# Second layer's attention: projection pieces moved to the odd steps and tied behind the scores

## The chip, the cores and the metric

The kernel runs on one core of one Trainium2 chip. The metric is device time in microseconds (us) of one execution. Engines are named as in the profile: PE (matrix multiply, PEld its weight loads), DVE (vector), ACT (scalar activation), POOL (the third elementwise engine), SP (its queue issues most DMAs).

## The reference, cut to what matters

A two-layer trunk over 512 latent tokens and 256 context tokens, width 1024. The second layer's mixer is windowed grouped-query attention with sinks: 16 query heads in 4 groups share 4 key/value heads of 64.

```python
def gqa_sink_attend(q, k, v, mask, sinks):
    ...
    s = jnp.einsum('bqkgd,bnkd->bkgqn', qg, k).astype(jnp.float32) * (HEAD_DIM ** -0.5)
    if mask is not None:
        s = jnp.where(mask, s, NEG_INF)
    ...
    p = jax.nn.softmax(jnp.concatenate([s, sink], axis=-1), axis=-1)[..., :-1]
    o = jnp.einsum('bkgqn,bnkd->bqkgd', p.astype(v.dtype), v)
    return o.reshape(B, Q, GQA_HEADS, HEAD_DIM)

def mixer_c(h_x, h_c, w_in, w_out, sinks, cos, sin, with_ctx_out):
    q_x, k_x, v_x = jnp.split(h_x @ w_in, [C_Q_COLS, C_Q_COLS + C_KV_COLS], axis=-1)
    q_x = apply_rope(heads(q_x, GQA_HEADS), cos, sin)
    ...
    out_x = block_sweep(blk, q_x).reshape(B, S, C_Q_COLS) @ w_out
```

Each block of 128 queries sees all 256 context keys and the latent keys of its own and the neighbouring blocks (256 or 384 keys).

## The kernel before, in words

Everything is kept with features on the partitions. An fp32 operand is split into a high and a low part, and a projection is three products per 128 features (`mm3`, line 205): high x high, high x low, low x high. A q projection for one pair of heads has 8 k-slices, so 24 matmuls on 512 columns; an output-projection piece over the first half of the features has 4 k-slices, so 12.

**Attention in steps.** Head pair `m` (0 to 7) and query block `i` (0 to 3) make 32 steps, `n = 4 m + i` (`gqa_step`, line 1525). A step has two parts. Part `a`, for both heads of the pair: scores on PE into a PSUM tile `s` (two buffers, one used per head; L1540 for context keys, L1542 for latent keys), mask and negated maximum on DVE (L1544), exponential with its sum on ACT (L1549), the sink's exponential (L1551), sum and reciprocal on DVE (L1553, L1554), normalising on POOL (L1557). Part `b`: transposes of the probabilities on PE into tiles `t` (L1569; a fifth block on L1581 in the middle query blocks), copies to SBUF by ACT (L1577, L1582) and DVE (L1575), and in every second step the value product for two query blocks together (`values`, L411), whose result is split into `att(m)` (L196 on ACT, L197 on DVE).

**Order.** `run_steps` (line 439) writes, for step `n`: part `a` of step `n`, part `b` of step `n - 1`, then the fillers of step `n`. So at even `n` the part `b` carries a value product, at odd `n` only transposes. The program builder decides each engine's issue order ahead of time: it plays the program through, and where an engine would be free it takes the earliest instruction of the source that is ready there. On the chip each engine then runs its list in order. `tc.issue_after(x)` makes the builder put what is written under it, on the engine of `x`, behind `x`; it sets an order and adds no wait for `x` to finish.

**Fillers.** `q_piece(m)` (line 1508) projects the queries of head pair `m`: weights from the stream `S`, `mm3` into the single PSUM tile `lin`, then rope (`rope_of`: DVE L386 and L387, POOL L388 and L389) and the split into `qs[m]` (ACT L369, DVE L372; four buffers). `first_part(t)` makes two output-projection pieces (`wo1`, L1618 adds them to the residual) over the features of head pairs 0 to 3, which are ready after step 15. Head pairs 4 to 7 write their results over `hx`, the input of the q pieces, so all q pieces come before these. Each `S.next()` loads weights (512 KB by SP), and prepares tiles up to two ahead: a cast on ACT (L158) and a subtraction on DVE (L159), into three buffers each.

The plan before spreads, per head pair, its pieces over the pair's four steps: q1 and q2 at steps 0 and 2, q3 and q4 at 4 and 6, q5 at 8, q6 at 12, q7 at 16, and the output pieces at 20, 22, 24 to 28 and 30. q0 comes before the steps. After the steps the second half of the output projection follows (four more weight tiles), then the norm and the FFN.

Of the kernel before, what the change touches and what calls it, by code (L numbers as in the profile page):

```python
# [15 lines left out]
P = 128  # L16
D = 1024
KT = D // P
NX = 512
NC = 256  # L20
# [17 lines left out]
def tile_trunk(  # L38
# [27 lines left out]
    nc = tc.nc  # L66
# [126 lines left out]
    S = Stream()  # L193

    def split(hi, lo, src, scale=1.0):
        nc.scalar.activation(hi, src, AF.Copy, scale=scale)  # L196
        return nc.vector.tensor_sub(lo, src, f32(hi))  # L197
# [4 lines left out]
        nc.gpsimd.dma_start(f32(lo), src, accum_op=ALU.add)  # L202
        nc.scalar.copy(hi, src)

    def mm3(ps, wh, wl, xh, xl, n=KT):
        for k in range(n):
            nc.tensor.matmul(ps, wh(k), xh(k), start=k == 0, stop=False)  # L207
            nc.tensor.matmul(ps, wh(k), xl(k), start=False, stop=False)  # L208
            end = nc.tensor.matmul(ps, wl(k), xh(k), start=False, stop=k == n - 1)  # L209
        return end  # L210
# [17 lines left out]
    def wslice(t, m=P):  # L228
        v = t.rearrange("p (k m) -> p k m", m=m)
        return lambda k: v[:, k, :]  # L230
# [127 lines left out]
    xh = lambda k: hx[k][:, 0, :]  # L358
    xl = lambda k: hx[k][:, 1, :]
# [76 lines left out]
    def vload():  # L436
        return [tuple(wslice(t, 256) for t in S.next()) for _ in range(2)]

    def run_steps(steps, fillers):

        prev = None
        for n, (a, b) in enumerate(steps):
            a()
            if prev:
                prev()
            prev = b
            for f in fillers[n] if n < len(fillers) else []:
                f()
        prev()

    def spread(items, n):
        out_ = [[] for _ in range(n)]
        for i, f in enumerate(items):
            out_[i * n // len(items)].append(f)
        return out_
# [172 lines left out]
    with ExitStack() as st:  # L628
# [3 lines left out]
        linp = lambda: lin.tile([P, NX], F32, tag="lin", name="lin")  # L632
# [32 lines left out]
        with ExitStack() as s0:  # L665
# [7 lines left out]
            def ada0_mm(b):  # L673
                ps = tp()
                for k in range(KT):
                    ada_mm(ps, S.next(0), k, k == 0, k == KT - 1)
                    S.request(min(S.at + 8, 2 * KT + 3))
                return ps
# [8 lines left out]
            ps = ada0_mm(0)  # L687
# [393 lines left out]
        ps = linp().rearrange("p (t c) -> p t c", t=2)  # L1081
# [47 lines left out]
        def first_part(t):  # L1129
            def f():  # L1130
                w = S.next()
                for m in (2 * t, 2 * t + 1):
                    wo_chunk(m, w, "x", 0)
                    wo_chunk(m, w, "c", 0)
            return f

        steps, fillers = [], []
# [31 lines left out]
        for t in range(4):  # L1169
            w = S.next(3)  # L1170
# [29 lines left out]
    with ExitStack() as st:  # L1200
# [17 lines left out]
        q_tile = lambda: fp.tile([P, 4 * H], F32, tag="q", name="q")  # L1218
# [198 lines left out]
        for n, sg in enumerate(supers0):  # L1417
            for p in sg:
# [9 lines left out]
                else:  # L1428
# [9 lines left out]
                    z, u = z_tile(), s_tile()  # L1438
# [14 lines left out]
    with ExitStack() as st:  # L1453
# [6 lines left out]
        linp = lambda: lin.tile([P, NX], F32, tag="lin", name="lin")  # L1460
# [11 lines left out]
        def q_tile(m, ps):  # L1472
            qs[m] = gp.tile([P, 2, NX], F32R, tag="gq", name="gq", bufs=4)
            evac_pair(qs[m], 0, NX, rope_of(ps, gp), -0.125)
# [33 lines left out]
        def q_piece(m):  # L1508
            def f():
                wh, wl = (wslice(t) for t in S.next())  # L1510
                ps = linp() if m else tp()
                mm3(ps, wh, wl, xh, xl)
                q_tile(m, ps)
            return f

        def att(m):

            if m < 4:
                return hc[2 * m], hc[2 * m + 1]
            return [hx[m][:, i, :].rearrange("p (a n) -> p a n", a=2) for i in range(2)]  # L1520
# [4 lines left out]
        def gqa_step(m, i):  # L1525
            kv = m // 2
            lo, hi = max(i - 1, 0), min(i + 1, 3)
            nk = (hi - lo + 1) * P
            d = {}

            def a():
                q = qs[m]
                small = lambda name: gp.tile([P, 2], F32, tag=name, name=name, bufs=4)
                mx, rs, es = small("mx"), small("rs"), small("es")
                pp = []
                for c in range(2):
                    ql = q[:, c, i * P : (i + 1) * P]
                    s = sps.tile([P, 1024], F32, tag="s", name="s")
                    for n, k in ((0, k1), (1, k2)):
                        nc.tensor.matmul(s[:, 256:512], ql, k[:, kv, 0:NC], start=(n == 0), stop=(n == 1))  # L1540
                    for n, k in ((0, k1), (1, k2)):
                        nc.tensor.matmul(s[:, 512 : 512 + nk], ql, k[:, kv, NC + lo * P : NC + lo * P + nk], start=(n == 0), stop=(n == 1))  # L1542
                    sv = s[:, 256 : 512 + nk]
                    nc.vector.tensor_tensor_reduce(  # L1544
                        out=sv, in0=sv, in1=gm0 if i == 0 else gm[:, 0 : 256 + nk], op0=ALU.add, op1=ALU.min,
                        scale=1.0, scalar=snk[:, 2 * m + c : 2 * m + c + 1], accum_out=mx[:, c : c + 1],
                    )
                    p = gp.tile([P, 640], F32, tag="p", name="p", bufs=5)
                    nc.scalar.activation(p[:, 0 : 256 + nk], sv, AF.Exp, bias=mx[:, c : c + 1], scale=-1.0, accum_out=rs[:, c : c + 1])  # L1549
                    sk = 2 * m + c  # L1550
                    nc.scalar.activation(es[:, c : c + 1], snk[:, sk : sk + 1], AF.Exp, bias=mx[:, c : c + 1], scale=-1.0)  # L1551
                    pp.append(p)
                nc.vector.tensor_add(rs, rs, es)  # L1553
                nc.vector.reciprocal(rs, rs)  # L1554
                for c in range(2):
                    z = pp[c][:, 0 : 256 + nk]
                    nc.gpsimd.tensor_scalar(z, z, rs[:, c : c + 1], 1.0, op0=ALU.mult, op1=ALU.mult)  # L1557
                d["p"] = pp

            def b():  # L1560
                nb = 2 + hi - lo + 1
                h = i % 2
                if h == 0:
                    turned[0] = gp.tile([P, 2, 10, P], F32, tag="pt", name="pt", bufs=1)
                pt = turned[0]
                for c in range(2):
                    t = tp((P, 4, P))
                    for k in range(4):
                        nc.tensor.transpose(t[:, k, :], d["p"][c][:, k * P : (k + 1) * P], ident)  # L1569
                    if i == 0:  # L1570
                        z, t = pt[:, c, 0:6, :].rearrange("p (a b) n -> p a b n", b=3)[:, :, 0:2, :], t.rearrange("p (a b) n -> p a b n", b=2)
                    else:
                        z = pt[:, c, 5 * h : 5 * h + 4, :]
                    if c:
                        nc.vector.tensor_copy(z, t)  # L1575
                    else:
                        nc.scalar.copy(z, t)  # L1577
                if nb == 5:
                    t = tp((P, 4, P))
                    for c in range(2):  # L1580
                        nc.tensor.transpose(t[:, c, :], d["p"][c][:, 4 * P : 5 * P], ident)  # L1581
                    nc.scalar.copy(pt[:, :, 5 * h + 4, :], t[:, 0:2, :])  # L1582
                if h == 0:
                    return
                o = tp()
                both = slice(0, 2 * P)

                def term(k, n, cols):
                    return (lambda c: v[:, k, 64 * kv : 64 * kv + 64], lambda c: pt[:, c, n, :], cols)


                values(o, [
                    term(0, slice(0, 6, 5), both),
                    *([term(i, 2, slice(0, P))] if i > 1 else []),
                    term(1 + i, slice(3, 8, 4), both),
                    term(2 + i, slice(4, 9, 4), both),
                    *([term(3 + i, 9, slice(P, 2 * P))] if i < 3 else []),
                    term(1, slice(1, 7, 5), both),
                ])
                split(*(z[:, i // 2, :] for z in att(m)), o[:, both])  # L1600

            return a, b


# [25 lines left out]
        for m in range(KT):  # L1630
# [2 lines left out]
        super_weights(1, type("", (), {"tile": lambda self, *a, **k: spool[0].tile(*a, **k)})())  # L1633
        q_piece(0)()
        steps, fillers = [], []
        plan = {
            0: [q_piece(1), q_piece(2)], 1: [q_piece(3), q_piece(4)], 2: [q_piece(5)], 3: [q_piece(6)], 4: [q_piece(7)],
            5: first_part(0), 6: first_part(1) + first_part(2), 7: first_part(3),
        }
        for m in range(8):  # L1640
            steps += [gqa_step(m, i) for i in range(4)]
            fillers += spread(plan[m], 4)
        run_steps(steps, fillers)
        held = []
        for t in range(4):
            w = S.next(0 if t >= 2 else 2)
# [336 lines left out]
```

## Time and profile before

| what | us |
|---|---|
| median of 3 runs | 1601.86 |
| lowest, highest | 1600.62, 1605.14 |
| the profiled execution | 1608.56 |
| its span | 1606.8 |
| mean granted PE clock in it | 0.991 |
| first scores to end of the last value product, in it | 1039.4 to 1216.6 |

The profiled execution is a run of its own, and its time stands beside the median of others. In the table by windows each row gives a stretch, then for each engine the busy time and the number of instructions, then the granted PE clock (1.00 is full), the DMA share and GB/s. A timeline row gives start, duration, engine, line, operation, tiles (out<-in), count, and in brackets the idle time before it with what ended it. A waits row says who waited on which line for whom: total us, times, longest. A groups row gives line, engine, tiles, shapes, count, then busy us and mean ns of one, then idle time before.

### The profile page before, as it was taken

To read this page: it belongs to the slowest core of one execution; us is meant where nothing else is said; L and a number is where in the kernel's file an instruction comes from. 1 tells how busy PE (TensorE), PEld (TensorE's weight loads), DVE (VectorE), ACT (ScalarE), POOL (GpSimd) and SP (SyncE) were. 2 spreads that over 40 slices of the span, in tenths; PEclk is the share of its full clock that TensorE was granted. 3 is DMA by queue.
4 is the path that set the end of the run, shared out by engine and by line. 5 is a ranking of instruction groups with operands and counts; after the bars stand their busy time and mean duration, and the time that the engine had idled before them with its cause. 6 is when DMAs were issued, how large, how long until landed. Compare 5 with 4: busy or idle time off the path is not lost.

```text
span 1606.8 us, 25479 instructions
## 1 busy us (share of the span) xinstructions
PE 1541.8 (96%) x9854; PEld 1377.4 (86%) x9854; DVE 1242.9 (77%) x2125; ACT 734.1 (46%) x1276; POOL 275.9 (17%) x311
## 2 busy tenths in 40 slices
PE   5899999999999999999999999999998999999997
PEld 3798888877878998999999998886777899989897
DVE  4667798966698789879798867677766987869686
ACT  4346545445344413434424254466664543525354
POOL 2222223463010000010100001354331000000001
PEclk9999999999999999999999999999999999999999
DMA  9312354543145465485866652320011442423321
GB/s 348 100 53 70 99 157 136 182 128 101 63 132 158 118 173 155 133 221 154 213 183 162 201 146 71 106 66 27 15 40 54 131 144 68 131 72 100 118 80 53
DMA packets 68577, 195.28 MB, mean 122 GB/s; under 512 B 6772, under 2 KB 19220, under 8 KB 68456
## 3 DMA queue, kind: packets, MB, share of 16 engines
q1 hardware_dynamic: 58824, 161.26, 31.5%
q0 software_dynamic: 9056, 31.87, 9.4%
q8 instruction: 78, 1.28, 0.3%
q10 hardware_dynamic: 576, 0.52, 0.1%
q14 instruction: 43, 0.35, 0.1%
HBM read 160.45 MB, written 4.86 MB: 103 GB/s over the span
## 4 chain that ended last, share of the span: by engine, by line
PE 52%; DVE 5%; DMA 4%; issue 4%; ACT 1%; POOL 0%; DVEq 0%; POOLq 0%; ACTq 0%; SPq 0%
PE f L1764 4%; PE f L1763 4%; PE f L1762 4%; PE f L1334 4%; PE f L1333 4%; PE f L1332 4%; PE f L1374 3%; PE f L1375 3%; PE f L1373 3%; PE t L411 2%; PE f L1815 2%; PE f L1817 2%; PE f L1816 2%; DMA wl<-raw 2%; PE t L1569 2%
## 5 line engine op out<-in xcount | busy, mean ns | idle before, releaser
L196 ACT ACTIVATE wh<-raw 128x1024 fp32r<-128x1024 f32 (+1 forms) x96 | 92.3, 978 | 232.4 <-DVE raw L540 106.6
L207 PE MATMUL lin<-hb,wh 128*128 128x512 f32 (+1 forms) x456 | 162.1, 356 | 8.3 <-DVE rbuf L387 2.1
L208 PE MATMUL lin<-hb,wh 128*128 128x512 f32 (+1 forms) x456 | 160.3, 351 | 1.0 <-DVE hb L1106 0.7
L209 PE MATMUL lin<-hb,wl 128*128 128x512 f32 (+1 forms) x456 | 158.4, 347 | 0.0
L197 DVE TENSOR_TENSOR wl<-raw,wh 128x1024 fp32r<-128x1024 f32 (+1 forms) x96 | 107.1, 1122 | 36.3 <-ACT wh L196 34.3
L269 DVE SCALAR_TENSOR_TENSOR junk<-raw,tables 128x1024 bf16<-128x1024 f32 x80 | 98.6, 1233 | 19.2 <-DMA raw<-in_ada_wT_dram 18.7
L202 POOL DMA_DIRECT2D wl<-raw x39 | 34.0, 872 | 445.3 <-ACT wl L201 412.0
L207 PEld LDWEIGHTS lin<-hb,wh 128*128 128x128 f32 x456 | 86.3, 189 | 23.9 <-issue 2.8
L1373 PE MATMUL f<-g,wh 128*128 128x512 f32 (+1 forms) x304 | 103.0, 340 | 0.6 <-DVE s L1362 0.6
L1374 PE MATMUL f<-g,wh 128*128 128x512 f32 (+1 forms) x304 | 102.9, 339 | 0.0
L1763 PE MATMUL f<-hb,wh 128*128 128x256 f32 x360 | 101.8, 284 | 0.0
L1762 PE MATMUL f<-hb,wh 128*128 128x256 f32 x360 | 101.6, 283 | 0.0
L1764 PE MATMUL f<-hb,wl 128*128 128x256 f32 x360 | 101.4, 284 | 0.0
L1375 PE MATMUL f<-g,wl 128*128 128x256 f32 (+1 forms) x304 | 100.8, 337 | 0.0
L1334 PE MATMUL f<-hb,wl 128*128 128x384 f32 x288 | 96.5, 335 | 1.0 <-DMA wl<-raw 1.0
L208 PEld LDWEIGHTS lin<-hb,wh 128*128 128x128 f32 x456 | 86.5, 190 | 12.4 <-DVE hb L1106 1.4
L159 DVE TENSOR_TENSOR wl<-raw,wh 128x1024 fp32r<-128x1024 f32 x61 | 80.7, 1325 | 20.6 <-ACT wh L158 20.3
L1332 PE MATMUL f<-hb,wh 128*128 128x384 f32 x288 | 96.4, 335 | 0.0
L1333 PE MATMUL f<-hb,wh 128*128 128x384 f32 x288 | 96.4, 335 | 0.0
L209 PEld LDWEIGHTS lin<-hb,wl 128*128 128x128 f32 x456 | 86.5, 190 | 10.8
L158 ACT CAST wh<-raw 128x1024 fp32r<-128x1024 f32 x61 | 63.9, 1048 | 67.0 <-PE t L208 15.0
L339 POOL TENSOR_TENSOR ns_a<-ns_a,ns_s 128x256 f32<-128x256 f32 (+1 forms) x16 | 17.9, 1118 | 433.7 <-ACT ns_s L335 427.0
(395 smaller groups left out, 4851.3 us busy)
## 6 DMA issues: line engine op xcount, KB each, us to landing
raw<-in_w_dram SPq DMA_DIRECT2D x132, 512.0 KB, 3.7
raw<-in_ada_wT_dram SPq DMA_DIRECT2D x80, 512.0 KB, 3.8
wl<-raw POOLq DMA_DIRECT2D x39, 512.0 KB, 6.3
raw<-in_w_ab_dram SPq DMA_DIRECT2D x24, 512.0 KB, 4.2
raw<-in_ada_w_dram SPq DMA_DIRECT2D x16, 512.0 KB, 9.5
raw<-in_w_c_dram SPq DMA_DIRECT2D x12, 512.0 KB, 4.4
nb<-in_na_bias_dram POOLq DMA_DIRECT2D x16, 256.0 KB, 3.2
raw<-in_wo_ab_dram SPq DMA_DIRECT2D x8, 512.0 KB, 3.7
```

The costliest lines, as they stand in the source:

```text
L207: nc.tensor.matmul(ps, wh(k), xh(k), start=k == 0, stop=False)
L208: nc.tensor.matmul(ps, wh(k), xl(k), start=False, stop=False)
L209: end = nc.tensor.matmul(ps, wl(k), xh(k), start=False, stop=k == n - 1)
L1332: nc.tensor.matmul(ps, wh(k), b[:, 0, :], start=k == 0, stop=False)
L1333: nc.tensor.matmul(ps, wh(k), b[:, 1, :], start=False, stop=False)
L1334: nc.tensor.matmul(ps, wl(k), b[:, 0, :], start=False, stop=k == 3)
L1373: nc.tensor.matmul(ps, hi, g[:, 0, cols[v]], start=first, stop=False)
L1374: nc.tensor.matmul(ps, hi, g[:, 1, cols[v]], start=False, stop=False)
L1375: nc.tensor.matmul(ps, lo, g[:, 0, cols[v]], start=False, stop=last)
L1762: nc.tensor.matmul(ps, wh(k), b[:, 0, :], start=k == 0, stop=False)
L1763: nc.tensor.matmul(ps, wh(k), b[:, 1, :], start=False, stop=False)
L1764: nc.tensor.matmul(ps, wl(k), b[:, 0, :], start=False, stop=k == 3)
```

## The change

Three things. `run_steps` takes `pin`, and from step 3 on (`n > 2`) writes the fillers of a step under `tc.issue_after` of the last score matmul traced so far, which is that of the same step's second head (`scored[0]`); only PE instructions are held by it. `q_halves(m)` makes a q piece in two halves of 12 matmuls on the same `lin` tile and weights; rope and split come with the second half. And the plan is a new one: q1 at step 0, then one item at each odd step and none at even ones: q2, q3, q4 at steps 1, 3, 5; the halves of q5 at 7 and 9; those of q6 at 11 and 13; q7 at 15; the eight output pieces at 17, 19, ... 31. `mm3` gets a list of k-slices for the halves. The arithmetic and its order within each sum stay the same.

```diff
-    def mm3(ps, wh, wl, xh, xl, n=KT):
-        for k in range(n):
+    def mm3(ps, wh, wl, xh, xl, n=KT, ks=None):
+        for k in ks or range(n):
...
-    def run_steps(steps, fillers):
+    def run_steps(steps, fillers, pin=None):
...
-            for f in fillers[n] if n < len(fillers) else []:
-                f()
+            with tc.issue_after(pin[0].ins) if pin and n > 2 else nullcontext():
+                for f in fillers[n] if n < len(fillers) else []:
+                    f()
...
+        def q_halves(m):
+            d = {}
+
+            def f(i):
+                if i == 0:
+                    d["w"] = [wslice(t) for t in S.next()]
+                    d["ps"] = linp()
+                mm3(d["ps"], *d["w"], xh, xl, ks=range(4 * i, 4 * i + 4))
+                if i:
+                    q_tile(m, d["ps"])
+
+            return [lambda i=i: f(i) for i in range(2)]
...
+        scored = [None]
...
-                        nc.tensor.matmul(s[:, 512 : 512 + nk], ql, k[:, kv, NC + lo * P : NC + lo * P + nk], start=(n == 0), stop=(n == 1))
+                        scored[0] = nc.tensor.matmul(s[:, 512 : 512 + nk], ql, k[:, kv, NC + lo * P : NC + lo * P + nk], start=(n == 0), stop=(n == 1))
...
-        plan = {
-            0: [q_piece(1), q_piece(2)], 1: [q_piece(3), q_piece(4)], 2: [q_piece(5)], 3: [q_piece(6)], 4: [q_piece(7)],
-            5: first_part(0), 6: first_part(1) + first_part(2), 7: first_part(3),
-        }
         for m in range(8):
             steps += [gqa_step(m, i) for i in range(4)]
-            fillers += spread(plan[m], 4)
-        run_steps(steps, fillers)
+        odd = [q_piece(m) for m in range(2, 5)] + q_halves(5) + q_halves(6) + [q_piece(7)]
+        odd += [f for t in range(4) for f in first_part(t)]
+        fillers = [f for z in odd for f in ([], [z])]
+        fillers[0] = [q_piece(1)]
+        run_steps(steps, fillers, scored)
```

## The prediction

> **What bounds the kernel now.** I read the page first, for the totals.
>
> ```profile
> span 1606.8 us, 25479 instructions
> ...
> PE 1541.8 (96%) x9854; PEld 1377.4 (86%) x9854; DVE 1242.9 (77%) x2125; ACT 734.1 (46%) x1276; POOL 275.9 (17%) x311
> ```
>
> PE is busy for 96% of the span, so the change can only win where PE stands in the attention of the second layer. No matmul goes away. Next I asked for busy time in four stretches from the first projection beside the attention (1033.3) to its last value product (1216.6), cut where the pieces come and go, and then for the same stretches counting only instructions on tile `lin`, the PSUM tile of the pieces.
>
> ```profile
> core 0: us, PE busy (x) PEld busy (x) DVE busy (x) ACT busy (x) POOL busy (x), PEclk, DMA share, GB/s
> 1033.30:1093.40 60.10, 58.83 (x325) 47.60 (x323) 46.32 (x90) 33.23 (x73) 33.92 (x28) 1.00 0.24 74
> 1093.40:1146.30 52.90, 47.48 (x339) 37.18 (x339) 39.37 (x99) 37.44 (x100) 19.39 (x24) 0.94 0.04 12
> 1146.30:1189.30 43.00, 43.00 (x285) 34.56 (x284) 29.76 (x66) 24.20 (x62) 15.48 (x16) 1.00 0.14 41
> 1189.30:1216.60 27.30, 23.32 (x186) 17.41 (x184) 16.40 (x46) 17.72 (x50) 8.79 (x12) 1.00 0.04 16
> ```
>
> ```profile
> 1033.30:1093.40 60.10, 39.90 (x165) 30.34 (x164) 8.09 (x18) 0.00 (x0) 1.00 0.24 74
> 1093.40:1146.30 52.90, 5.58 (x15) 2.96 (x16) 2.15 (x4) 0.00 (x0) 0.94 0.04 12
> 1146.30:1189.30 43.00, 20.77 (x84) 15.36 (x84) 5.24 (x7) 0.00 (x0) 1.00 0.14 41
> 1189.30:1216.60 27.30, 0.00 (x0) 0.00 (x0) 0.00 (x0) 0.00 (x0) 1.00 0.04 16
> ```
>
> Call the stretches A, B, C, D. The pieces (264 matmuls) do not lie where the plan of the source puts them: 165 are used up in A, 15 fall in B, 84 in C, none in D. The order was taken as early as the pieces were ready, and B and D run attention alone.
>
> To see what that costs I need the pure work. The pace of piece matmuls, and two neighbouring pairs of steps in C (from one value product to the next), each with 24 piece matmuls:
>
> ```profile
> 1041.82 0.40 PE L208 MATMUL lin<-hb,wh 128*128 128x512 f32 x1
> ...
> 1046.83 0.39 PE L209 MATMUL lin<-hb,wl 128*128 128x512 f32 x1
> ```
>
> ```profile
> 1161.37:1173.22 11.85, 11.85 (x80) 9.71 (x79) 8.33 (x20) 6.80 (x18) 4.00 (x4) 1.00 0.16 44
> 1173.22:1185.08 11.86, 11.86 (x80) 9.71 (x79) 7.99 (x17) 6.62 (x18) 3.79 (x4) 1.00 0.15 46
> ```
>
> The two rows are the 2nd and the 24th matmul of a piece: 5.01 / 22 = 0.2277 us each, so a q piece (24) is 5.46 us and an output piece or a q half (12) is 2.73. A pair without its pieces is then 11.86 - 5.46 = 6.40 us (6.39 on the mean of both). A pair has 16 score, 18 transpose and 20 value matmuls, 54 in all. Work in A: 160 / 54 x 6.39 + 165 x 0.2277 = 56.5, so 3.6 us lost; B: 324 / 54 x 6.39 + 15 x 0.2277 = 41.8, 11.1 lost; C: 42.9, 0.1 lost; D: 186 / 54 x 6.39 = 22.0, 5.3 lost. In all **20.1 us** of lost PE time, and C shows that pieces beside the steps can take the loss to nothing. Per pair it is 1.85 in B (6.0 pairs), 1.54 in D (3.44 pairs), 0.03 in C.
>
> What ends the waits, from the waits of PE in B (first row) and in D (the other two):
>
> ```profile
> PE s L1540 <- ACT p L1549: 4.4, 6, 1.3
> ...
> PE s L1540 <- ACT p L1549: 2.9, 4, 0.9
> PE t L411 <- DVE pt L1575: 0.9, 1, 0.9
> ```
>
> Scores wait for the exponential that frees their PSUM tile (two buffers). That chain is late partly because PE itself had starved it: at the end of A the piece for q7 was issued ahead of a value product, and the followers show how long they stood:
>
> ```profile
> 1095.95 0.76 DVE L1544 CUSTOM_DVE_ANT_0 s<-s,gm,snk 128x512 f32<-128x512 f32 x1 [5.21 <-PE s L1542]
> ...
> 1095.63 0.38 ACT L196 ACTIVATE hb<-t 128x256 fp32r<-128x256 f32 x1 [5.77 <-PE t L411]
> ```
>
> Part of B's loss is the clock:
>
> ```profile
> 1100.00:1102.00 2.00, 0.85 (x4) 0.53 (x4) 1.97 (x6) 1.31 (x5) 1.28 (x1) 0.89 0.00 0
> 1102.00:1104.00 2.00, 1.91 (x6) 1.62 (x7) 2.00 (x6) 0.55 (x3) 1.79 (x1) 0.50 0.00 0
> 1104.00:1106.00 2.00, 1.78 (x8) 1.27 (x8) 1.29 (x6) 1.24 (x4) 1.64 (x3) 0.50 0.85 252
> 1106.00:1108.00 2.00, 2.00 (x10) 1.95 (x9) 0.76 (x2) 1.50 (x4) 1.36 (x2) 0.50 0.07 18
> ```
>
> The granted clock is 0.89, then 0.50 for 6 us: 0.2 + 3.0 = 3.2 of B's 11.1 us. No wait in B was longer than 1.3 us. The Trainium skill, page "TensorE: Matmul & The Clock Gate", section "What's actually happening", has the array fall to half rate after an idle window of some 3.4 us; by that letter no drop should stand here, only the waits would be there to win, and 3.2 us would stay in the sum (gain 3.7 instead of 6.9). The row decides: the drop came, in a stretch where PE stood for over half of 2 us, and it should go with the stretch.
>
> **The change part by part.** It removes no instruction and adds none; it moves pieces. q1 to q4 go to steps 0, 1, 3, 5; q5 and q6 in halves to 7, 9 and 11, 13; q7 to 15; the eight output pieces to 17 to 31. So 12 pairs get 12 piece matmuls and 4 get 24. The tie holds a piece's matmuls behind the last score matmul of its step: issue order only. Queued behind them on PE is whatever comes later in the order; who waits is the rope or the residual of that piece, both with steps in hand. What is lost after, term by term:
>
> *Start.* A's 3.6 us stays. Steps 2 and 3 add to it: q3 may not start before the scores of step 3. A step's softmax, in C:
>
> ```profile
> 1169.34 0.48 PE L1540 MATMUL s<-gk,gq 128*128 128x256 f32 x2
> ...
> 1170.10 0.76 DVE L1544 CUSTOM_DVE_ANT_0 s<-s,gm,snk 128x512 f32<-128x512 f32 x1
> ...
> 1171.01 0.69 ACT L1549 ACTIVATE p<-s,mx 128x512 f32<-128x512 f32 x1 [1.02 <-DVE mx L1544]
> ...
> 1173.46 2.42 POOL L1557 TENSOR_SCALAR p<-p,rs 128x512 f32<-128x512 f32 x2 [2.35 <-DVE rs L1554]
> ...
> 1173.22 2.17 PE L411 MATMUL t<-pt,gv 128*64 128x256 f32 x20
> 1175.32 1.09 PE L1569 MATMUL t<-ident,p 128*128 128x128 f32 x8
> ```
>
> Scores to a free score tile: 1171.70 - 1169.34 = 2.4 us; two such turns are 4.7, with a step's 2.15 us of scores and transposes (6.39 less the value product's 2.10, halved) and half of the next's in them: 0 to 2 us, I take 1.5.
>
> *Twelve pairs with one piece.* From scores to their transposes 1175.32 - 1169.34 = 6.0 us pass. In an odd step PE has, until it needs those, 2.15 + 2.73 + about 1.1 (the next step's scores) = 6.0: no or little wait. An even step has no piece, and between its transposes and its value product stands a copy, whose wait with nothing in between is
>
> ```profile
> 1214.46 2.17 PE L411 MATMUL t<-pt,gv 128*64 128x256 f32 x20 [0.88 <-DVE pt L1575]
> ```
>
> So 0 to 0.88 a pair; scores of the next step can go in between when their tile is free, so about half: 0.4 x 12 = 4.8 us. By the nearest other rows it is 0.03 (C) to 1.54 (D) a pair.
>
> *Four pairs with a whole q piece:* as C, 0.1.
>
> *Rope of q5, q6, q7.* It comes now where cover is thin.
>
> ```profile
> L389 POOL TENSOR_TENSOR rt<-rt,ru 128x512 f32<-128x512 f32 x8 | 15.5, 1935 | 0.8 <-DVE rt L387 0.3
> L388 POOL TENSOR_TENSOR ru<-ru,tables 128x512 f32<-128x512 f32 x8 | 10.3, 1286 | 23.2 <-DVE ru L386 23.2
> ...
> 1092.30:1108.79 16.49, 13.94 (x73) 10.64 (x72) 10.67 (x25) 8.89 (x22) 6.25 (x7) 0.79 0.18 60
> ```
>
> POOL is held 1.94 + 1.29 = 3.2 us, ahead of the normalising that the transposes wait for. The last row is the one place with a rope and little cover: 73 matmuls, 7 of them pieces, are 9.4 us of work, 7.1 lost; less the clock's 3.2 and B's usual waits it leaves about 1.4 a rope. Bounds 0 to 4.2 for three; I take 2.0.
>
> *End.* The last piece now lies in step 31 and covers part of the drain, but the weight tile that it frees is wanted in the next stage: 0.7 to 2, I take 1.2.
>
> *Weights.* Their order is the same, they are prepared two tiles ahead, and now later:
>
> ```profile
> raw<-in_wo_c_dram SPq DMA_DIRECT2D x8, 512.0 KB, 3.6
> ...
> 1161.25 1.04 ACT L158 CAST wh<-raw 128x1024 fp32r<-128x1024 f32 x1
> ...
> 1162.41 1.22 DVE L159 TENSOR_TENSOR wl<-raw,wh 128x1024 fp32r<-128x1024 f32 x1
> ```
>
> 3.6 + 1.04 + 1.22 = 5.9 us, against at least a pair of steps (9.1) of cover: nothing; 5.9 once if a tile came without it.
>
> Sum: 3.6 + 1.5 + 4.8 + 0.1 + 2.0 + 1.2 = 13.2 us lost after, 20.1 before: **6.9 us saved**. The profiled execution took 1608.56 us (span 1606.8 and 1.8 around it), so 1601.7; the median of the runs is 1601.86, 6.7 below that execution, and the same saving gives **1595.0**. With all lower ends the loss is 4.8 (gain 15); with all upper ones (0.88 a pair) 22.8 (2.7 slower).
>
> **Rivals.** (1) *Full cover.* The 12 pairs run as C: nearly all lower ends, about 1587. For: C's 0.03. Against: C has two pieces a pair, one of them ahead of the value product. (2) *No difference.* The issue order, fixed ahead of time, still puts each piece in one block ahead of work that feeds the other engines, as before 1095, or new waits at start, ropes and even steps take what B and D give back: about 1601. That is 0.9 us a pair in place of 0.4. (3) *Slower.* The tie itself: a piece behind scores that wait for the exponential cannot fill that wait, and every pair pays D's 1.54 in spite of its piece: 3.6 + 1.5 + 18.5 + 0.1 + 2.0 + 1.2 = 26.9, 6.8 more than now, 1608.7. It decides above (20.1 - 8.4) / 12 = 0.98 us a pair. For: ten such waits in B and D. Against: a piece of 2.73 us moves the next scores back by more than those waits (at most 1.3). The Trainium skill, same page, section "Step-by-step: what each phase is for", says that matmuls stay in program order, which is what (3) needs; the trace agrees so far as PE stood at 1100 with pieces left.
>
> **How the numbers follow.** Forecast 0.51, (1) 0.17, (2) 0.18, (3) 0.14. About 0.3%, 4.8 us, can be told from no change here. The forecast's own range is 1590 to 1600; 0.41 of it is faster than that bound, 0.10 within. Faster 0.41 + 0.17 = 0.58, same 0.10 + 0.18 = 0.28, slower 0.14. The range takes in (1) and (2) and leaves out (3): 1586 to 1605.
>
> **What would show it.** Right: piece matmuls in every pair to the end; the stretch from the first scores to the last value product 5 to 9 us shorter; granted clock 1.00 throughout; waits of scores on the exponential below half of 7.3 us. Wrong: those waits as long as before; waits of transposes on POOL at steps 9 to 16 of several us; a gap of over 2 us at steps 2 and 3; or a difference that lies outside 1033 to 1217.

## The result, and the profile after

The kernel after the change takes 1619.29 us (median of 4 runs, 1618.65 to 1620.28), the kernel before 1603.5 (1600.62 to 1605.74): ratio 1.0096, 95% interval 1.0083 to 1.0109. It is slower by 1%, where 0.4% faster was forecast, and above the range. The medians lie 15.8 us apart and the two profiled executions only 11.7 (1608.56 and 1620.28): the one before was 5.1 us above its median, the one after 1.0. What follows is read from these two.

The totals of the page after; as before, PE does the same 9854 matmuls:

```profile
span 1618.5 us, 25450 instructions
...
PE 1542.5 (95%) x9854; PEld 1378.7 (85%) x9854; DVE 1242.1 (77%) x2125; ACT 734.3 (45%) x1276; POOL 271.0 (17%) x311
```

The stretch from q1's first matmul to the last value product grew from 183.3 to 196.7 us; what lies outside it changed by under 2 us (1423.5 before, 1421.8 after). I cut the stretch at events that both kernels have: q1's first matmul, the first value product, the ninth, the last one's end. First the kernel before, then after; columns as in the prediction's window tables.

```profile
1033.29:1063.45 30.16, 28.90 (x143) 23.53 (x141) 24.28 (x45) 17.30 (x34) 16.99 (x13) 1.00 0.31 95
1063.45:1149.16 85.71, 80.28 (x533) 63.36 (x533) 63.13 (x150) 55.63 (x147) 37.78 (x42) 0.96 0.09 26
1149.16:1216.60 67.44, 63.46 (x456) 49.88 (x455) 44.44 (x106) 39.67 (x104) 22.81 (x27) 1.00 0.11 32
```

```profile
1030.78:1065.59 34.81, 28.41 (x127) 23.01 (x125) 22.41 (x46) 16.89 (x37) 16.13 (x14) 0.85 0.24 67
1065.59:1157.28 91.69, 82.60 (x550) 65.50 (x549) 64.69 (x149) 56.03 (x144) 38.34 (x41) 0.98 0.09 30
1157.28:1227.45 70.17, 63.10 (x456) 50.70 (x455) 43.70 (x106) 39.94 (x104) 20.02 (x27) 1.00 0.10 30
```

The same rows counting only tile `lin`, after (before it was 96, 97 and 73 piece matmuls):

```profile
1030.78:1065.59 34.81, 19.46 (x72) 14.80 (x71) 3.10 (x8) 0.00 (x0) 0.85 0.24 67
1065.59:1157.28 91.69, 29.25 (x120) 22.06 (x120) 6.96 (x15) 0.00 (x0) 0.98 0.09 30
1157.28:1227.45 70.17, 17.51 (x73) 13.28 (x72) 5.22 (x7) 0.00 (x0) 1.00 0.10 30
```

With the prediction's prices (6.39 us for 54 attention matmuls, 0.2277 for a piece matmul) the lost time by stretch before is 2.7, 12.0 and 5.5 us, after 11.9, 13.5 and 8.2. So of 13.4 us more, **9.2 lie at the start, 1.5 in the middle and 2.7 at the output pieces**. The pieces did spread as planned (the first stretch has 24 fewer). Nothing was gained where they went. The busy time of PE in the three rows rose by only 1.5 us (172.6 to 174.1), its idle time by 11.9 (10.7 to 22.6): the loss is waiting. The waits of PE in the whole stretch, after:

```profile
PE s L1558 <- ACT p L1567: 18.0, 15, 3.0
PE t L411 <- DVE pt L1593: 2.5, 3, 1.3
```

Scores (L1558 is the old L1540) wait 18.0 us for the exponential, before 7.3 (4.4 and 2.9 in B and D): 10.7 of the 11.9 us. The start, on PE, then ACT, then DVE's share:

```profile
1047.93 0.51 PE L1558 MATMUL s<-gk,gq 128*128 128x256 f32 x2 [1.12 <-ACT p L1567]
...
1051.82 0.80 PE L1558 MATMUL s<-gk,gq 128*128 128x256 f32 x2 [3.04 <-ACT p L1567]
...
1055.22 0.79 PE L1558 MATMUL s<-gk,gq 128*128 128x256 f32 x2 [1.11 <-ACT p L1567]
```

```profile
1049.58 1.28 ACT L369 ACTIVATE gq<-rt 64x512 fp32r<-64x512 f32 x2 [1.52 <-POOL rt L389]
1050.88 0.79 ACT L1567 ACTIVATE p<-s,mx 128x640 f32<-128x640 f32 x1
```

```profile
1045.00:1050.00 5.00, 2.66 (x18) 2.02 (x16) 5.00 (x9) 2.71 (x6) 4.47 (x4) 1.00 0.16 13
1050.00:1055.00 5.00, 2.29 (x8) 1.97 (x8) 3.91 (x10) 3.58 (x10) 0.55 (x1) 0.57 0.23 92
1055.00:1060.00 5.00, 4.78 (x13) 3.99 (x14) 1.71 (x6) 1.50 (x7) 2.59 (x4) 0.50 0.00 0
```

From q2's end to q3's first matmul (1044.6 to 1056.2) PE has only the scores of steps 1 to 3 and one step's transposes. DVE is busy for all of 1045 to 1050, ACT stands before q2's split with an exponential queued behind it, PE is about half busy (2.66 and 2.29 of 5 us), and the granted clock falls to 0.50, at which most of q3 then runs. Further on, the place that repeats in the output pairs:

```profile
1171.87 1.04 PE L1587 MATMUL t<-ident,p 128*128 128x128 f32 x8
1172.74 0.38 PE L1599 MATMUL t<-ident,p 128*128 128x128 f32 x2
1173.93 0.51 PE L1558 MATMUL s<-gk,gq 128*128 128x256 f32 x2 [0.81 <-ACT p L1567]
...
1174.60 2.17 PE L411 MATMUL t<-pt,gv 128*64 128x256 f32 x20
1176.70 0.51 PE L1558 MATMUL s<-gk,gq 128*128 128x256 f32 x2
```

After the transposes that the even step carries, only the odd step's first scores are left; their tile still holds the even step's, PE stands for the exponential, then come the value product and the second head's scores, and only behind those the piece. Waits of the same scores stand ahead of value products in the middle stretch as well, where q halves were to fill them:

```profile
1085.81 0.51 PE L1558 MATMUL s<-gk,gq 128*128 128x256 f32 x2 [1.94 <-ACT p L1567]
...
1096.62 0.50 PE L1558 MATMUL s<-gk,gq 128*128 128x256 f32 x2 [0.92 <-ACT p L1567]
...
1108.20 0.50 PE L1558 MATMUL s<-gk,gq 128*128 128x256 f32 x2 [1.50 <-ACT p L1567]
```

### The profile page after: what moved, and what is told of

It is laid out like the page before. It is cut to its first block, busy times and chain, and to the rows that moved or that the text cites. A ratio compares the mean times of both kernels' runs of the same rounds, so it can differ in the third digit from the quotient of the medians.

```text
span 1618.5 us, 25450 instructions
## 1 busy us (share of the span) xinstructions
PE 1542.5 (95%) x9854; PEld 1378.7 (85%) x9854; DVE 1242.1 (77%) x2125; ACT 734.3 (45%) x1276; POOL 271.0 (17%) x311
## 4 chain that ended last, share of the span: by engine, by line
PE 54%; DVE 5%; issue 3%; DMA 3%; ACT 2%; POOL 1%; DVEq 0%; POOLq 0%; ACTq 0%; SPq 0%
PE f L1336 4%; PE f L1335 4%; PE f L1334 4%; PE f L1782 4%; PE f L1783 4%; PE f L1781 4%; PE f L1376 3%; PE f L1375 3%; PE f L1377 3%; PE f L1834 2%; PE f L1835 2%; PE f L1836 2%; PE t L411 2%; DMA wl<-raw 1%; PE f L207 1%
```

## The experiments

The theories. **H, the hole:** the tie together with empty even steps leaves a place ahead of each value product that no piece may fill. **S, the start:** the tie of q3 uncovers the softmax of steps 1 to 3. Against them: **T**, any tie costs, wherever it is; **P**, the new plan or the halves cost by themselves; **R** and **Q**, the rope and split behind a q piece make the scores late; **L**, the softmax's chain alone does. For the runs with q7 in halves: **B**, the block of q7's matmuls ahead of a value product starves the other engines. Each run is given with its median and its ratio to runs of the kernel before on the same chip.

**Without the tie.**

```diff
-        run_steps(steps, fillers, scored)
+        run_steps(steps, fillers)
```

> The change with its new plan and halves, but without the tie. Theory H (the tie, with even steps left empty, opens a hole that no piece may fill): without the tie the pieces go early again, in the same runs as before the change (24 beside each of the first steps, 3 here and there until 12s come after step 16, none at the end), so the time is that of before, 1603 within 0.3%, and scores wait on the exponential for about 7 us as before. Theory P (the new plan or the halves cost by themselves, as weights come later or a piece is cut): 1612 to 1619.

1604.27 us beside 1604.61, ratio 0.9993 (0.9984 to 1.0003): no difference. The builder's order is that of before in all but a few places, and so are the waits:

```profile
PE s L1558 <- ACT p L1567: 7.6, 11, 1.3
```

P falls. Plan and halves do nothing without the tie; it is the tie that makes them act.

**The old plan with the tie alone.**

```diff
+            with tc.issue_after(pin[0].ins) if pin and n > 2 else nullcontext():
...
+        scored = [None]
...
-        run_steps(steps, fillers)
+        run_steps(steps, fillers, scored)
```

> The plan of before with whole pieces, mostly at even steps, with the tie alone added from the fourth step on. Theory T (the tie costs wherever the pieces lie, because scores that wait hold the piece back): as slow as the change, 1615 to 1620. Theory H: the pieces now lie in even steps, where the hole is, so the waits of scores on the exponential fall under those of the change (18 us) by half or more, and the time is 1596 to 1608; the long stand of the change at steps 1 to 3 stays in part, since q3 waits for step 4.

1624.09, ratio 1.0123 (1.0103 to 1.0143): above both expectations. Its interval between value products with the largest loss, and two waits:

```profile
1099.57:1119.73 20.16, 15.78 (x78) 12.36 (x77) 12.32 (x29) 10.21 (x28) 7.76 (x8) 0.75 0.09 27
```

```profile
PE s L1543 <- ACT p L1552: 12.7, 9, 3.1
PE t L411 <- DVE pt L1578: 7.8, 6, 1.9
```

The old plan has four steps from q5 to q6 and from q6 to q7; tied, the steps between run with little or no piece beside them, in the interval shown at a clock of 0.75 on the mean. But where its output pieces lie at even steps, the value products follow each other in 9.1 to 9.2 us with one piece and 11.8 to 11.9 with two (their starts: 1171.55, 1180.70, 1192.55, 1204.41, 1213.49, 1222.61), which is the pure work of 9.1 and 11.9. So T's mechanism falls there, though its total was nearer; H missed too, by 16 us and in the waits (12.7, where 9 or less was expected): it left out the gaps that the tie opens between whole q pieces.

**Even steps.**

```diff
         fillers = [f for z in odd for f in ([], [z])]
-        fillers[0] = [q_piece(1)]
+        fillers = fillers[1:] + [[]]
+        fillers[0] = [q_piece(1)] + fillers[0]
+        fillers[14], fillers[15] = [], fillers[14]
```

> The change with its pieces moved one step earlier, to even steps (q7 alone stays at step 15), still tied to their own step's scores. Theory H: the piece lies between the scores of the even step and the transposes and value product that wait, so the waits of scores on the exponential drop from 18 us to 6 or less and the time comes to 1590 to 1600, faster than before. Theory T: it stays at 1612 to 1620.

1611.35, ratio 1.0041 (1.0025 to 1.0056), between the two: 11 us above H's range and just under T's. The waits of the scores went as H said, others came, which H had not foreseen:

```profile
PE t L411 <- DVE pt L1593: 5.9, 6, 1.9
PE t L411 <- ACT p L1567: 3.1, 3, 2.7
PE s L1558 <- ACT p L1567: 2.3, 4, 0.8
```

**Tied behind the step before.**

```diff
+            tie = pin[0] if pin and n > 2 else None
             a()
...
-            with tc.issue_after(pin[0].ins) if pin and n > 2 else nullcontext():
+            with tc.issue_after(tie.ins) if tie else nullcontext():
```

> The change with odd steps kept, but each piece tied behind the last scores of the step before its own, so that it may come forward by one step, into the even one. Theory H: the hole can be filled, 1590 to 1602. Theory T: a tie is still there, 1612 to 1620. The start (scores of steps 1 to 3 waiting 1.1, 3.0 and 1.1 us in the change) should be nearly gone too, as q3 may start after step 2's scores.

1611.74, ratio 1.0048 (1.0029 to 1.0066): half the loss is gone, but the time is 10 us above H's range and only 0.3 under T's. The trace says more than the time. Two like pairs of steps with one output piece, in the change and then in this kernel:

```profile
1164.26:1174.60 10.34, 9.53 (x67) 7.79 (x66) 6.42 (x16) 5.29 (x16) 2.93 (x4) 1.00 0.01 2
1174.60:1185.03 10.43, 9.13 (x68) 7.51 (x67) 7.09 (x18) 6.94 (x19) 2.93 (x4) 1.00 0.08 18
```

```profile
1152.74:1161.83 9.09, 9.09 (x68) 7.48 (x67) 6.93 (x17) 5.07 (x14) 2.02 (x3) 1.00 0.19 59
1181.49:1190.50 9.01, 9.01 (x68) 7.48 (x67) 5.92 (x15) 5.96 (x17) 3.16 (x4) 1.00 0.01 2
```

The change's pairs are 1.2 to 1.3 us above the pure work of 9.1, these are at it. The middle stretch takes 88.79 us (91.69 in the change), the output pieces' 67.35 (70.17). The start stayed, against the expectation (34.0 us to the first value product, 34.8 in the change): q3 may now follow step 2's scores, but those are the ones that wait longest, and q3 behind them.

```profile
PE s L1559 <- ACT p L1568: 6.2, 6, 3.1
```

**The tie only from the eighth step on.**

```diff
-            with tc.issue_after(pin[0].ins) if pin and n > 2 else nullcontext():
+            with tc.issue_after(pin[0].ins) if pin and n > 6 else nullcontext():
```

> The change with the tie only from the eighth step on, so q1 to q4 go as early as before. Theory S (a third of the change's loss is its start: between the end of q2's matmuls and q3's first one PE waits 1.1, 3.0 and 1.1 us for the exponential and runs on at half clock): the stretch up to the first value product loses about 2 us in place of 11, q3 and q4 are then missing beside steps 3 to 6, and the time is 1609 to 1614. Theory H (the start does not matter, the hole in the even steps is all): 1617 to 1620.

1612.0, ratio 1.0040 (1.0028 to 1.0053), as S said. The start of this kernel:

```profile
1031.78:1061.98 30.20, 28.94 (x143) 23.51 (x141) 24.30 (x45) 17.32 (x34) 17.02 (x13) 1.00 0.33 95
```

30.20 us with 143 matmuls, where before has 30.16 with 143 and the change 34.81 with 127: the loss of the start is that of before. Some 7 us of the change's loss come from there (1619.29 less 1612.0): by the prices above 9.1 are saved at the start, and 1.3 come back in the middle stretch, where q3 and q4 are then missing.

**Rope of the q pieces on DVE.**

```diff
-        nc.gpsimd.tensor_mul(u, u, sint)
-        nc.gpsimd.tensor_add(t, t, u)
+        eng.tensor_mul(u, u, sint)
+        eng.tensor_add(t, t, u)
```

(`eng` is DVE for q pieces, POOL elsewhere.)

> The change with the two POOL operations of the q pieces' rope (1.28 and 2.14 us) put on DVE (some 0.7 us each); the same results. Theory R (ACT stands before a q tile's split, waiting for POOL, with the exponentials that free the score tiles queued behind it): the 3.0 us wait at the start falls to about 1.5 and the pairs with the ropes of q5 to q7 lose 1 us less each, 1611 to 1616. Theory D (DVE is as full as POOL's chain is long, 1.4 us more a piece): 1618 to 1622.

1622.08, ratio 1.0109 (1.0094 to 1.0124). R's gain doesn't come, as theory D said. At the start the longest wait of scores does fall, from 3.0 to 1.8 us, and the stretch from 34.81 to 33.33. But DVE has the work instead, the middle stretch takes 95.12 us in place of 91.69, and in sum the scores wait about as long as in the change:

```profile
PE s L1559 <- ACT p L1568: 17.5, 16, 2.5
```

**Without the rope** (left out for q2 to q7, so this kernel does not compute the reference).

```diff
-            evac_pair(qs[m], 0, NX, rope_of(ps, gp), -0.125)
+            evac_pair(qs[m], 0, NX, rope_of(ps, gp) if m < 2 else ps, -0.125)
```

> The change with the rope left out of q2 to q7 (the split reads the projection itself: 1.4 us of DVE and 3.4 of POOL fewer a piece, so the output isn't the reference's). Theory Q (what follows a q piece on DVE, ACT and POOL makes the late scores: DVE was busy for 5.0 of 5 us at the start): the stretch to the first value product loses 7 or less in place of 11 and q5 to q7 cost 1 to 2 us less each, 1609 to 1614. Theory L (the softmax's own chain, with no piece beside it, sets the waits): 1616 to 1620.

1615.48, ratio 1.0068 (1.0053 to 1.0082), between the two theories; the trace tells them apart. The start is

```profile
1030.57:1062.66 32.09, 27.15 (x128) 21.97 (x126) 19.75 (x41) 16.62 (x37) 12.78 (x12) 0.89 0.25 74
```

2.7 us shorter than in the change (34.81). From the first to the last value product it takes 1062.66 to 1222.32, the change 1065.59 to 1225.30: 159.7 both. So the ropes cost 2.7 us at the start and, in sum, nothing later. What stays of the start's loss, about 9 us by the same sum, speaks for L for the most part: the softmax of steps 1 to 3 without cover, and the clock. The split of the q pieces is still in it, and no run takes that apart.

**Both repairs:** tied behind the step before, from the eighth step on (the two diffs above together).

> The change with both repairs: pieces tied behind the step before their own, and only from the eighth step on. If the two terms add (start about 8 us, hole about 7 us), 1602 to 1605, the time of before. If one is hidden by the other, 1608 to 1612.

1609.01, ratio 1.0026 (1.0016 to 1.0037). Each repair alone gave back 7.3 and 7.6 us of 15.8; together it is 10.3, and the time is in the range set for one hiding the other, not in that of a full sum. Not even then is the spread of the q pieces worth anything over before.

**Only the output pieces spread.** The q pieces at their steps of before and free, the first output piece free at step 17; pieces 2 to 8 at steps 19 to 31, tied behind the step before, the last two (29, 31) behind their own.

```diff
-            tie = pin[0] if pin and n > 2 else None
+            tie = pin[0] if pin and n > 17 else None
...
+            with tc.issue_after((pin[0] if n > 28 else tie).ins) if tie else nullcontext():
```

> The kernel before with its free, whole q pieces and free first output piece; only the other seven output pieces are spread over steps 19 to 31 and tied behind the scores of the step before their own. Theory H: the attention-alone end of the kernel before (some 7 us lost over its last four pairs and the drain) goes to 2 or 3 us, nothing else changes, 1597 to 1601 beside 1604 before. Theory T (a tie costs wherever it is): 1606 or more. In between it is no difference: the end without a piece takes back what the middle gives.

1603.45 beside 1604.85, ratio 0.9991 (0.9982 to 1.0000): no difference, and less than expected. The stretch of the output pieces went from 67.44 to 65.74 us, 1.7 of the 4 to 5 that H gave it. Scores still wait 6.0 us, 4.6 of it in the middle stretch, which this edit leaves alone.

**The same, all tied behind their own step.**

```diff
-            with tc.issue_after((pin[0] if n > 28 else tie).ins) if tie else nullcontext():
+            with tc.issue_after(pin[0].ins) if tie else nullcontext():
```

> The same kernel as the one with seven output pieces spread, but all of these tied behind the scores of their own odd step, as in the change, in place of the step before (the last two were that already). Theory H: five pairs with an empty even step lose 1.2 to 1.9 us each in place of about 0.4, so 4 to 7 us slower than that kernel, 1606 to 1611. Theory T: no difference between the two ties, 1602 to 1605.

1607.56, ratio 1.0019 (1.0009 to 1.0028), 4.1 us above the kernel it was made from. This is the cleanest pair: same plan, same pieces, the tie one step apart. Two like pairs of steps, first tied to the step before, then to their own step:

```profile
1153.29:1162.41 9.12, 9.12 (x68) 7.60 (x67) 6.23 (x17) 6.50 (x17) 2.43 (x5) 1.00 0.01 2
1172.95:1181.96 9.01, 9.01 (x67) 7.47 (x67) 5.91 (x15) 5.96 (x17) 3.17 (x4) 1.00 0.01 2
```

```profile
1151.68:1162.00 10.32, 9.51 (x68) 7.78 (x67) 6.41 (x16) 5.29 (x16) 2.95 (x4) 1.00 0.01 2
1172.45:1182.77 10.32, 9.51 (x66) 7.97 (x67) 6.19 (x16) 5.57 (x17) 2.95 (x4) 1.00 0.09 36
```

9.0 to 9.1 us against 10.32 for 54 + 12 matmuls, 1.2 to 1.3 us a pair. The whole stretch from the ninth value product to the end of the last takes 65.74 and 70.45 us, the two stretches ahead of it the same in both (30.16 and 30.20, 84.81 and 84.86). That is H, alone.

**q7 in halves as well.** The kernel with seven output pieces spread, and q7 in halves tied behind the step before, at steps 9 and 11 or at 10 and 12 (q6 is moved to step 8, free).

```diff
-        for m, n in ((1, 0), (2, 2), (3, 4), (4, 6), (5, 8), (6, 12), (7, 16)):
+        for m, n in ((1, 0), (2, 2), (3, 4), (4, 6), (5, 8), (6, 8)):
             fillers[n].append(q_piece(m))
+        for n, f in zip((9, 11), q_halves(7)):
+            fillers[n].append(f)
...
-            tie = pin[0] if pin and n > 17 else None
+            tie = pin[0] if pin and (n > 17 or n in (9, 11)) else None
```

> The kernel with seven output pieces spread, and q7 also cut into halves at steps 9 and 11, tied behind the step before. In the kernel before, 21 matmuls of q7 stand ahead of a value product for which ACT and DVE wait over 5 us, and that pair loses 7 us with the clock. Theory B (the block starves the other engines): 3 to 5 us less, 1598 to 1601. Theory Q (rope and split set it wherever the matmuls lie): 1602 to 1605.

> The same with the halves at steps 10 and 12, so that a piece lies in one more pair without any. Theory B: 1597 to 1601. Theory Q: 1602 to 1605.

1598.18, ratio 0.9961 (0.9946 to 0.9977), and 1599.44, ratio 0.9966 (0.9952 to 0.9979): both faster than the kernel before and than the one they were made from, as theory B said. The middle stretch takes 80.56 and 80.87 us, in that kernel 84.81; start and end are the same within 0.4 us. Where the kernel before lost 7 us in the pair from 1092.30, the waits of scores in the whole stretch are now (halves at 9 and 11)

```profile
PE s L1559 <- ACT p L1568: 2.1, 4, 0.8
```

## Why the prediction was wrong

*What bounds the kernel*: right in kind. The loss of 20.1 us by stretches holds, and so does the price of work (9.1 us for a pair with one piece, in four kernels). But only 10.7 us of the loss was idle time of PE, 7.3 of it waits of scores on the exponential; the rest lay in matmuls that took longer than their price. The lost time after was summed up to 13.2 us and came out as 33.6 (11.9, 13.5 and 8.2). Two signs of being wrong that I had named came: longer waits of scores, and a gap of 3.0 us at steps 2 and 3.

*Twelve pairs with one piece, 0.4 us each*: this step failed. Three like pairs with an output piece in the change take 10.3 to 10.4 us, 1.2 to 1.3 over the work, nearly as much as a pair without any piece loses (D's 1.54). The four with a q half take 11.0 to 12.1, 1.9 to 2.9 over it. I took the odd step's wait to be covered (it is) and half of the even step's to be filled by scores of the next step. Those were the very instructions that stood, because their PSUM tile was not free, and the tie behind the second head's scores kept the piece from taking their place. I had written that as rival 3, with D's 1.54 a pair and the point 0.98 from which it decides, and gave it 0.14; its 1608.7 was still 10.6 us too low. What I set against it, that a piece moves the next scores back by more than such a wait, is true of the even step's scores, which come behind the piece, and not of the odd step's, which come ahead of it. The pair of kernels that differ by one step of the tie shows the mechanism for the output pieces. For the q halves it is read from the waits ahead of their value products (1.94, 0.92 and 1.50 us) and from the 2.9 us that the tie to the step before took off the middle stretch.

*Start, 1.5 us*: failed by more. It is 9.2. I counted two turns of the softmax at their pace in C; here q2's rope, split and weights share DVE (busy 5.0 of 5 us), and the clock halves. The run with the free start gives it back; by the run without rope 2.7 us of it are the rope's.

*Rope, 2.0 us*: nothing in sum at q5 to q7 by the run without rope, 2.7 at the start, where I had not looked for it. Its 1.4 a rope does not come out of its figures either: 7.1 less 3.2 less B's 1.85 is 2.05. *Weights*: no wait of PE in this stretch is for a weight tile. *Four full pairs, 0.1*: too low for q4's, which takes 12.82 us with 24 piece matmuls, 1.0 over the work; tied to the step before it takes 11.92. *End, 1.2*: not told apart. (The upper ends add up to 22.5, not 22.8.) *Clock*: I expected 1.00 throughout; it fell again, at the start (0.85 over 34.81 us, 5.2 us) and a little in the middle (0.98, 1.8 us), against 3.4 before. These products of share and length are upper bounds, as the clock also falls while PE waits. The pair from 1092.30, which took 16.49 us with 3.5 lost to the clock in this way, ran at full clock in the kernel with the output pieces alone spread:

```profile
1087.88:1103.51 15.63, 11.68 (x74) 8.22 (x73) 10.62 (x25) 8.86 (x22) 6.28 (x7) 1.00 0.17 62
```

PE is 2.3 us less busy, the pair only 0.9 shorter. So of the 3.2 us of B that the forecast put down to the clock, the length of this pair shows only 0.9.

*Gain from B*: this failed too; the forecast took B's loss for a lack of pieces. Spread q pieces did not lower it (12.0 us in the middle stretch before, 13.5 after). The runs with q7 in halves gained 4 to 5 us over the kernel with q7 whole: that fits the size of the block that was issued ahead of a value product, as the rows of DVE and ACT at 1095 had said. But halves, tie and q6's place were changed together there, and no run takes them apart. With the tie to the step before, the middle stretch still loses 9.5 us by the same prices; what holds that part stays open.

That the change would act only through its tie was taken for granted; the run without it shows it.

## What to carry to other kernels

A piece of filler helps only where it may be issued at the moment when PE would stand, so find the instruction that waits, and tie the filler behind what lies ahead of *that*, not behind the waiting instruction itself. A tie one step earlier was worth 1.2 to 1.3 us a pair here, with nothing else changed. And a hole that a filler leaves behind counts at its new price: q3, which had been issued behind step 1's scores and was now held behind step 3's, cost more (9.2 us at the start, against 1.5 and 2.7 later).

## What the runs showed of the hardware

The granted clock fell to 0.50 for some us without any wait of PE as long as 3.4 us: before the change from about 1102, where PE had been busy for 1.8 of 4 us with waits of at most 1.3, and in the change from about 1051, in the middle of a wait of 3.0. The Trainium skill, page "TensorE: Matmul & The Clock Gate", section "What's actually happening", ties it to an idle window of about 3.4 us; no single wait in these two places is that long. The share of busy time does not decide it either. In the run without the tie the clock fell after four busier us, in the one with the tie from the eighth step on it stayed after four emptier ones:

```profile
1093.00:1097.00 4.00, 2.30 (x15) 1.68 (x13) 3.88 (x10) 3.95 (x10) 0.00 (x0) 1.00 0.00 0
1097.00:1099.00 2.00, 1.77 (x5) 1.25 (x6) 2.00 (x5) 1.25 (x6) 1.68 (x2) 0.60 0.00 0
```

```profile
1066.00:1070.00 4.00, 1.18 (x9) 0.74 (x7) 3.88 (x12) 3.33 (x9) 0.97 (x1) 1.00 0.37 131
1070.00:1072.00 2.00, 2.00 (x13) 1.60 (x14) 1.66 (x5) 0.99 (x5) 1.78 (x2) 1.00 0.00 0
```

What sets it stays open. Nor is it the same from one execution to the next: the kernel before, the one without the tie and the one with the output pieces alone spread have the same pair of steps in the middle, and it lost 3.5, 1.7 and 0.0 us to the clock, by share times length. It took 16.49, 15.79 and 15.63 us.
